# Dilated attention's values projected with tokens in the partitions, for several head pairs at once

## The chip, the cores and the metric

The kernel runs on one core of a Trainium2 chip. The metric is the device time of one execution in microseconds (us). Three runs of the kernel before gave 2261.0, 2262.21 and 2257.98; the median is 2261.0.

## The reference

Two decoder layers over 512 tokens of width 1024, in float32. Each layer is a half-step SwiGLU FFN, a token mixer and another half-step FFN, each between two RMSNorms and with shift, scale and gate computed from `c`. The first layer's mixer is latent attention; the second's is dilated attention, which the change is about:

```python
def dilated_attention(h, w_in, w_o, rel_bias):
    proj = (h @ w_in).reshape(B, S, N_GROUPS, 3, DIL_HEADS, DIL_HEAD_DIM)
    for g, (window, dilation) in enumerate(DIL_GROUPS):   # (128,1), (512,4), (2048,16)
        o, lse = strided_window_attention(
            proj[:, :, g, 0], proj[:, :, g, 1], proj[:, :, g, 2],
            dilation, window // dilation, rel_bias[:, g * DIL_HEADS:(g + 1) * DIL_HEADS])
    ...
    alpha = jax.nn.softmax(jnp.stack(lses, axis=0), axis=0)
    o = jnp.sum(alpha[..., None] * jnp.stack(outs, axis=0), axis=0)
    return o.reshape(B, S, DIL_WIDTH) @ w_o
```

There are three groups with 16 heads of 64 in each, every group with its own queries, keys and values. In group 0 a query sees the 128 tokens before it and itself, in group 1 every 4th token, in group 2 every 16th; a bias that depends on the distance is added to the scores. The three groups' results are joined by one softmax over all their scores.

## The kernel before, in words

The stages follow each other: FFN, latent attention, FFN, FFN, dilated attention (class `Dil`), FFN. All large products are made of three matmuls (`mm3`, L142): both operands are split into a part that TensorE's fp32r format holds and a rest, and high x high, high x low and low x high are added in PSUM. The lines L144, L145 and L146 are these three. A weight tile of 128x1024 is loaded by a DMA on SP's queue into one of 5 raw buffers, its high part is made by ACT (L129) and its rest by DVE in two halves (L131); `SLOTS` = 6 such pairs of tiles are in the ring.

The order of the instructions comes from a planner that estimates costs and puts each on its engine when it is ready, by its place in the program. Inside a `manual_schedule` block TensorE, ACT and DVE keep the order in which the program names them. SP's DMAs are always placed by the planner. The kernel has 44 SBUF tiles of 128x512 (`s`), four PSUM banks with the tag `mm` and four with `aux`. The normalized input `h` of a stage lies with the model dimension in the partitions and the 512 tokens along them, as 8 high and 8 low tiles. `x`, the residual stream, stays in SBUF the whole time (16 KB per partition).

The dilated stage goes by 8 pairs of heads. A pair has nine projections, one for each group and each of query, key and value (`tile`, L1032): 24 matmuls of 512 tokens, the weights being held in the array and `h` streaming, so that the result has the pair's 128 dimensions in the partitions. ACT copies it out of PSUM (L1061) and brings the tokens into the group's order; keys and values are written reversed (`back`), since the bias table is laid out for that. Products with the values need their tokens in the partitions. So every value tile is followed, one tile later, by four transposes of 128x128 on TensorE (L1071) and a copy by DVE (L1073).

One pair's attention stands beside the nine projections of the next pair (`slot`, L1279, and `beside`, L1300):

- slots 0 and 1: the scores (L1096) and, on DVE, bias and row minimum in one instruction (L1109). The minima of the three groups go out to DRAM and come back in another order (`tops_out`, L1135);
- tile 3: `tops` (L1142) joins them into one bound for all groups, which goes through DRAM again for groups 0 and 2;
- tiles 4 to 6: the exponentials and their sums on ACT (L1168), then the sums go through DRAM (`norm`, L1178);
- slots 7 and 8: transposes of group 0's weights (L1218) with their copies (L1230). Slot 0 of the next pair: those of group 1, and DVE's own 32x32 transposes for group 2 (L1232);
- slots 0 and 1 of the next pair: the products with the values (`weigh`, L1252), then the product with 1/sum (L1262), which comes by way of DRAM (`norm_out`, L1186).

`rest` (L1311) begins with the bias tables: a product (L971), a copy (L975), a DMA to DRAM (L976), and from there loads that put each head's table into a tile with shifted rows (L987). Pair 0's three value tiles follow, six other tiles having been made in the transition from the FFN before. `ahead` requests weights `LEAD` = 5 tiles in advance. At the end pair 7's scores come after the last tile, and the output projection (`part`, `tail`) runs beside its exponentials.

Of the kernel before, what the change touches and what calls it, by code (L numbers as in the profile page):

```python
# [14 lines left out]
P = 128  # L15
SEQ = 512
# [19 lines left out]
LEAD = 5  # L36
# [42 lines left out]
class Trunk:  # L79
    def __init__(self, ctx, tc, a):  # L80
# [11 lines left out]
        self.x = self.cp.tile([P, TT, D], F32, name="x")  # L92
# [14 lines left out]
        self.G = self.cp.tile([P, 2, 3, KT], F32, name="mG")  # L107

# [216 lines left out]
    def halves(self, i):  # L325
        return [self.x[:, i, d * SEQ : (d + 1) * SEQ] for d in range(2)]
# [10 lines left out]
    def start(self, sub):  # L337
# [16 lines left out]
        def stream(i):  # L354
            nc.sync.dma_start(self.x[:, i], self.a["x"][i])
# [137 lines left out]
    def tile_done(self, nxt, i):  # L493

        nc = self.nc
        r = self.scale_of(self.ss)
        for d in range(2):
            c = slice(d * SEQ, (d + 1) * SEQ)
            x = self.x[:, i, c]
# [22 lines left out]
class Ffn:  # L522
    heads = HEAD
    late = False
# [176 lines left out]
class Mla(Mixer):  # L701
    heads = 6
    late = True
# [245 lines left out]
class Dil(Mixer):  # L949
    heads = 6  # L950
    late = False
# [67 lines left out]
    ORDER = (0, 1, 3, 4, 6, 7, 2, 5, 8)  # L1019
# [12 lines left out]
    def tile(self, p, u, lo, hi):  # L1032
# [15 lines left out]
        if kind:  # L1048
            at = runs - at - part
        for q in range(1 if g < 2 else 4):  # L1050
            if g == 0:
                out, src = dst[:, at : at + part], b
            elif g == 1:
                out = dst.rearrange("p (r l) -> p r l", r=4)[:, :, at : at + part]
                src = self.order(b, 1)
            else:
                out = self.split(dst, 2)[:, q, :, at : at + part]
                src = self.order(b, 2)[:, q]
            if kind:
                src = self.back(src)  # L1060
            nc.scalar.activation(out, src, AF.Copy)  # L1061
# [15 lines left out]
    def scores(self, p, u, tag="mm"):  # L1077
# [26 lines left out]
        for e in range(2):  # L1104
            pair["y"][u, e] = y[e]
            at = 0
            for i, k0, n, b0 in blocks:
                c = slice(at, at + n)
                nc.vector.tensor_tensor_reduce(  # L1109
                    y[e][:, c],  # L1110
                    s[e][:, c],
                    pair["bias"][e][:, b0 : b0 + n],
# [110 lines left out]
    def turn_down(self, p, step, b):  # L1223
        t, nc = self.t, self.t.nc
        _, tag, pieces, _ = self.TURNS[step]
        out = self.pairs[p][step] = [t.t(tag) for e in range(2)]
# [7 lines left out]
    def weigh(self, p, step, first=0, last=3):  # L1234
# [5 lines left out]
        v = self.qkv[p, 3 * g + 2]  # L1240
        for nth, (kt, c0, n, at) in enumerate(products):
            for e in range(2):
# [6 lines left out]
                else:  # L1249
# [4 lines left out]
                    v[:, kt * P + 64 * e :][:, :64],  # L1254
# [5 lines left out]
        if step == last:  # L1260
            x = t.s()
            nc.vector.tensor_tensor(x, pair["acc"], pair["r"], ALU.mult)  # L1262
            self.of.append(x)

    def values(self, p, steps):
        for n in steps:
            self.weigh(p, n)

    def ahead(self, n):

        while self.coming and self.ahead_of < n:
            p, u = self.coming.pop(0)
            self.ahead_of += 1
            if p == "out":
                self.out_weights(u)
            else:
                self.wt[p, u] = self.t.weights(self.t.a["dil_in"][p, u])

    def slot(self, p, n):  # L1279

        if n == 0:
            if p:
                b = self.turn_up(p - 1, 2)
                self.values(p - 1, (0, 1))
            self.scores(p, 0)
            self.scores(p, 1)
            if p:
                self.turn_down(p - 1, 2, b)
                self.turn(p - 1, 3)
        elif n == 1:  # L1290
            if p:
                self.values(p - 1, (2, 3))
            self.scores(p, 2)
            self.scores(p, 3, "aux")
        elif n == 6:
            self.biases(p + 1)
        elif n > 6:
            self.turn(p, n - 7)

    def beside(self, p, n):  # L1300
        if n == 3:
            self.tops(self.pairs[p])
        elif n == 4:
            self.exps(p, (2,))
        elif n == 5:
            self.exps(p, (0, 1))
        elif n == 6:
# [3 lines left out]
    def rest(self):  # L1311
# [6 lines left out]
        tiles = [(0, u) for u in self.ORDER[6:]] + [(p, u) for p in range(1, 8) for u in self.ORDER]  # L1318
        self.coming = tiles + [("out", j) for j in range(PART)]
        self.ahead_of = 0  # L1320
        with t.tc.manual_schedule(engines={PE, ACT, DVE}):
            for at, (p, u) in enumerate(tiles):
                n = self.ORDER.index(u)
                if p:
                    self.slot(p - 1, n)
                if (p, n) == (7, 8):
                    self.scores(7, 0)
                self.ahead(at + LEAD)
                if p:
                    self.beside(p - 1, n)  # L1330
                self.tile(p, u, 0, SEQ)
                if p and n == 8:
                    self.norm_out(self.pairs[p - 1])
# [9 lines left out]
        self.scores(7, 2)  # L1343
        self.values(6, (2, 3))
        self.scores(7, 3)
# [3 lines left out]
        self.exps(7, range(4))  # L1349
        self.norm(self.pairs[7])  # L1350
        order = (2, 0, 1, 3)
        with t.tc.manual_schedule(engines={PE, DVE}):
# [9 lines left out]
            self.weigh(7, order[-1], order[0], order[-1])  # L1362
        self.put_o(self.of[-1])
# [29 lines left out]
def layout(i):  # L1393
# [52 lines left out]
    out["dil_in"] = tiles(w).reshape(8, 9, P, CH)  # L1446
    out["dil_o"] = c(g["dil_w_o"][0].reshape(KT, P, D))
# [31 lines left out]
```

## Time and profile before

| | |
|---|---|
| median of three runs | 2261.0 us |
| the profiled execution | 2258.17 us |
| its span, first to last instruction | 2256.1 us |
| granted TensorE clock, mean | 0.998 |
| TensorE busy in the span | 99% |
| DVE, ACT busy | 53%, 38% |
| transposes of value tiles (L1071) | 96, 14.6 us busy |
| DVE's copies behind them (L1073) | 24, 16.6 us busy |

A line of the view of groups names the source line, the engine, the operation, its output and inputs with the instruction's shape, and the count; then the busy time of the group, the mean time of one in ns, and the idle time of the engine before them with what ended it. `PE` is TensorE, `PEld` its weight load, which overlaps matmuls; matmuls are pipelined, so the distance from start to start says more than a duration. The chain of waits gives start, duration and the work that the end of the program hung on. A row of the stages has the window, its length, then busy time and count for PE, PEld, DVE, ACT and POOL, the granted clock, the share of the DMA engines and GB/s. `SPq` rows are DMAs as SP's queue issues them.

### The profile page before, as it was taken

The page shows a single profiled execution, that of the slowest core. Times are in us where ns is not written, and L with a number is a line of the kernel's source. Part 1 is how long each engine was busy: PE and PEld are TensorE (multiplying, and loading weights), DVE is VectorE, ACT ScalarE, POOL GpSimd, SP SyncE. Part 2 cuts the span into 40 slices and gives each one's busy share as a digit, 9 for nine tenths or more (in the row PEclk, how much of TensorE's full clock was granted, in tenths as well). Part 3 has the DMA queues.
Part 4 walks back from the last instruction along what each step waited for, and adds up shares of the span by engine and source line. Part 5 has one row for each costly group of instructions (what it writes and reads, how often), then busy time and mean ns, then how long its engine had stood idle before and what let it go on. Part 6 is the DMA issues. An engine that isn't in the chain of part 4 may idle for free.

```text
span 2256.1 us, 30214 instructions
## 1 busy us (share of the span) xinstructions
PE 2224.4 (99%) x11422; PEld 1853.9 (82%) x11422; DVE 1196.9 (53%) x2712; ACT 848.9 (38%) x1752; POOL 107.9 (5%) x143
## 2 busy tenths in 40 slices
PE   7999999999999999999999999999999999999998
PEld 5888888877898888898888888888888878888887
DVE  7666565677665356474554464343444467333344
ACT  4422234587633132353322252444444436322232
POOL 0000001210110000020000010000000002000000
PEclk9999999999999999999999999999999999999999
DMA  8575762311255365334553533333333322233231
GB/s 309 164 239 187 196 218 71 114 48 57 77 166 181 100 196 181 117 125 140 174 177 114 157 97 94 97 88 97 94 89 97 79 85 76 84 120 101 79 112 38
DMA packets 121224, 284.04 MB, mean 126 GB/s; under 512 B 44130, under 2 KB 48501, under 8 KB 121078
## 3 DMA queue, kind: packets, MB, share of 16 engines
q1 hardware_dynamic: 121078, 282.11, 41.0%
q8 instruction: 89, 1.46, 0.3%
q14 instruction: 57, 0.47, 0.1%
HBM read 279.67 MB, written 2.39 MB: 125 GB/s over the span
## 4 chain that ended last, share of the span: by engine, by line
PE 92%; issue 2%; ACT 2%; DVE 2%; DMA 1%; POOL 1%; SPq 0%; POOLq 0%; DVEq 0%; ACTq 0%
PE mm L144 28%; PE mm L145 28%; PE mm L146 28%; PE mm L863 1%; PE aux L1252 1%; PE mm L1096 1%; PE aux L1218 1%; PE aux L912 1%; POOL mv L319 1%; PE aux L891 1%; PE aux L513 1%; PE aux L1071 0%; ACT whi L129 0%; DVE x L500 0%; DMA d<-w 0%
## 5 line engine op out<-in xcount | busy, mean ns | idle before, releaser
L144 PE MATMUL mm<-s,whi 128*128 128x512 f32 (+1 forms) x2116 | 793.9, 376 | 2.7 <-ACT whi L129 2.4
L146 PE MATMUL mm<-s,wlo 128*128 128x512 f32 (+1 forms) x2116 | 790.0, 373 | 0.0
L145 PE MATMUL mm<-s,whi 128*128 128x512 f32 (+1 forms) x2116 | 790.0, 373 | 0.0
L131 DVE TENSOR_TENSOR wlo<-raw,whi 128x512 fp32r<-128x512 f32 (+1 forms) x712 | 466.6, 693 | 571.4 <-ACT whi L129 570.8
L129 ACT ACTIVATE whi<-raw 128x1024 fp32r<-128x1024 f32 (+1 forms) x356 | 369.1, 1052 | 789.4 <-PE mm L145 556.2
L144 PEld LDWEIGHTS mm<-s,whi 128*128 128x128 f32 x2116 | 398.4, 188 | 77.4 <-ACT whi L129 3.1
L146 PEld LDWEIGHTS mm<-s,wlo 128*128 128x128 f32 x2116 | 398.6, 188 | 70.8
L145 PEld LDWEIGHTS mm<-s,whi 128*128 128x128 f32 x2116 | 398.9, 189 | 68.7
L144 PE MATMUL mm<-whi,s 128*128 128x512 f32 x848 | 332.4, 392 | 2.8 <-DVE dm L1109 1.6
L145 PE MATMUL mm<-wlo,s 128*128 128x512 f32 x848 | 330.5, 390 | 0.0
L146 PE MATMUL mm<-whi,s 128*128 128x512 f32 x848 | 330.1, 389 | 0.0
L166 DVE CUSTOM_DVE_ANT_0 raw<-raw,cs 128x1024 f32<-128x1024 f32 x130 | 160.7, 1241 | 119.2 <-DMA raw<-w_mod 118.9
L144 PEld LDWEIGHTS mm<-whi,s 128*128 128x128 f32 x848 | 159.2, 188 | 37.0 <-issue 2.9
L146 PEld LDWEIGHTS mm<-whi,s 128*128 128x128 f32 x848 | 159.2, 188 | 33.3 <-issue 0.2
L145 PEld LDWEIGHTS mm<-wlo,s 128*128 128x128 f32 x848 | 159.2, 188 | 32.9 <-issue 0.5
L1061 ACT ACTIVATE s<-mm 128x512 f32<-128x512 f32 (+3 forms) x156 | 48.7, 370 | 261.4 <-PE mm L146 260.5
L460 DVE TENSOR_TENSOR s<-mm,s 128x512 f32<-128x512 f32 x112 | 76.7, 690 | 119.0 <-PE mm L146 118.8
L319 POOL TENSOR_TENSOR mv<-mv,mhalf 128x1 f32<-128x1 f32 x48 | 36.6, 763 | 1501.8 <-DVE mv L318 1499.3
L571 ACT ACTIVATE s<-gg 128x512 fp32r<-128x512 f32 (+1 forms) x97 | 57.4, 592 | 40.5 <-DVE gg L570 40.5
L570 DVE TENSOR_TENSOR gg<-silu,mm 128x512 f32<-128x512 f32 (+1 forms) x95 | 59.9, 630 | 10.3 <-ACT silu L568 10.3
L568 ACT ACTIVATE silu<-mm 128x512 f32<-128x512 f32 (+1 forms) x95 | 51.4, 541 | 15.8 <-PE mm L146 15.8
L145 PE MATMUL mm<-s 128*128 128x256 f32 (+1 forms) x176 | 52.9, 306 | 3.9 <-DVE s L308 2.3
(171 smaller groups left out, 1707.8 us busy)
## 6 DMA issues: line engine op xcount, KB each, us to landing
raw<-w_gu SPq DMA_DIRECT2D x168, 512.0 KB, 4.3
raw<-w_mod SPq DMA_DIRECT2D x130, 512.0 KB, 4.8
raw<-w_down SPq DMA_DIRECT2D x88, 512.0 KB, 4.3
raw<-dil_in SPq DMA_DIRECT2D x70, 512.0 KB, 3.7
s<-w_mod SPq DMA_DIRECT2D x28, 256.0 KB, 6.0
raw<-w_gu SPq DMA_DIRECT2D x16, 256.0 KB, 3.1
raw<-mla_o SPq DMA_DIRECT2D x8, 512.0 KB, 3.6
raw<-dil_o SPq DMA_DIRECT2D x8, 512.0 KB, 3.7
```

The source lines that it names most:

```text
L129: self.nc.scalar.activation(hi, raw, AF.Copy)
L131: self.nc.vector.tensor_tensor(lo[:, r], raw[:, r], f(hi[:, r]), ALU.subtract)
L144: mm(out, w[0], m[0], start=first, stop=False)
L145: mm(out, w[0], m[1], start=False, stop=False)
L146: mm(out, w[1], m[0], start=False, stop=last)
L166: nc.vector.tensor_tensor_reduce(raw, raw, self.cs, 1.0, 0.0, ALU.mult, ALU.add, accum_out=t[:, 0:1])
L319: nc.gpsimd.tensor_tensor(v[:, 1:2], v[:, 0:1], self.mhalf[:, 0:1], ALU.pow)
L460: nc.vector.tensor_tensor(y, b, y, ALU.add)
L568: nc.scalar.activation(s, banks[0], AF.Silu)
L570: nc.vector.tensor_tensor(v, s, banks[1], ALU.mult)
L571: nc.scalar.activation(ghi, v, AF.Copy)
L1061: nc.scalar.activation(out, src, AF.Copy)
```

## The change

Values of pairs 0 to 3 and of pairs 4 to 6 are projected together, with `h` held in the array as weights and the value weights streaming: for each group and each quarter of the tokens 24 matmuls over 512 or 384 columns. The result has its tokens in the partitions, and needs no transposes. For groups 1 and 2 the held operand is every 4th token of `h`; for group 2, four DMAs per quarter then bring the rows into the group's order. The twelve such tiles come behind the six query and key tiles that stand beside pair 0's and pair 4's attention. Pair 7's values are made as before, at the end.

The results need room: eight 128x512 pieces lie where `x` lies. `x` is now four tiles; in the transition to the dilated stage each is written to DRAM, and it is loaded back at the stage's end.

A pair's attention now stands beside six tiles. Values are no longer written reversed; DVE writes the scores reversed instead. All of `weigh` comes in slot 1, the transposes of groups 0 in slot 0 of the next pair.

```diff
-    ORDER = (0, 1, 3, 4, 6, 7, 2, 5, 8)
+    ORDER = (0, 1, 3, 4, 6, 7)
+    BLOCKS_V = {0: (0, 4), 4: (4, 7)}
+    LAST = (5, 2, 8)
...
+            if nxt.parks:
+                self.park(i)
+    def park(self, i):
+        to = self.parked[i] = self.dram.tile([P, D], F32, name=f"park{i}")
+        self.nc.sync.dma_start(to, self.x[i])
+    def unpark(self, i):
+        self.x[i] = self.wide()
+        self.nc.sync.dma_start(self.x[i], self.parked[i])
...
                 nc.vector.tensor_tensor_reduce(
-                    y[e][:, c],
-                    s[e][:, c],
-                    pair["bias"][e][:, b0 : b0 + n],
+                    self.back(o),
+                    a,
+                    b,
...
+    def keys_of(self, h, g, j):
+        return self.order(h, 1)[:, j] if g else h[:, j * P : (j + 1) * P]
+    def value_tile(self, p, g, j):
+        t, nc = self.t, self.t.nc
+        n = (self.BLOCKS_V[p][1] - p) * P
...
+        b = t.bank()[:, :n]
+        for k in range(KT):
+            w = [x[:, k % 2 * n :][:, :n] for x in self.wt[p, g, k // 2]]
+            h = [self.keys_of(x[k], g, j) for x in t.h]
+            t.mm3(b, h, w, k == 0, k == KT - 1)
+            if j == 3 and k % 2:
+                self.ahead(self.at + SLOTS + k // 2 + 1)
+        dst = self.made[g][j][:, :n]
+        out = t.s()[:, :n] if g == 2 else dst
+        nc.scalar.activation(out, b, AF.Copy)
+        if g == 2:
+            for a in range(4):
+                nc.sync.dma_start(
+                    dst[32 * a : 32 * a + 32], out.rearrange("(l a) v -> a l v", a=4)[a]
+                )
...
     def slot(self, p, n):
         if n == 0:
             if p:
-                b = self.turn_up(p - 1, 2)
-                self.values(p - 1, (0, 1))
+                up = [self.turn_up(p - 1, step) for step in range(2)]
+                for step in range(2):
+                    self.turn_down(p - 1, step, up[step])
             self.scores(p, 0)
             self.scores(p, 1)
             if p:
-                self.turn_down(p - 1, 2, b)
                 self.turn(p - 1, 3)
         elif n == 1:
+            if p == 7:
+                self.scores(p, 2)
+                self.scores(p, 3, "aux")
             if p:
-                self.values(p - 1, (2, 3))
-            self.scores(p, 2)
-            self.scores(p, 3, "aux")
-        elif n == 6:
+                for step in range(4):
+                    self.weigh(p - 1, step)
+            if p < 7:
+                self.scores(p, 2)
+                self.scores(p, 3, "aux")
+        elif n == 4:
             self.biases(p + 1)
-        elif n > 6:
-            self.turn(p, n - 7)
+        elif n == 5:
+            self.turn(p, 2)
     def beside(self, p, n):
-        if n == 3:
+        if n == 1 and p:
+            self.norm_out(self.pairs[p - 1])
+        elif n == 2 and p:
+            self.finish(p - 1)
+        elif n == 3:
             self.tops(self.pairs[p])
+            self.exps(p, (2,))
         elif n == 4:
-            self.exps(p, (2,))
-        elif n == 5:
             self.exps(p, (0, 1))
-        elif n == 6:
+    def behind(self, p, n):
+        if n == 5:
             self.exps(p, (3,))
             self.norm(self.pairs[p])
...
         with t.tc.manual_schedule(engines={PE, ACT, DVE}):
+            for p in range(7):
+                values = [(p, g, j) for g in range(3) for j in range(4) if p in self.BLOCKS_V]
+                for n, at in enumerate([(p + 1, u) for u in self.ORDER] + values):
+                    self.slot(p, n)
+                    self.ahead(self.at + min(SLOTS - 1 + max(n - 6, 0) % 4, SLOTS))
+                    self.beside(p, n)
+                    if n < 6:
+                        self.tile(*at, 0, SEQ)
+                    else:
+                        self.value_tile(*at)
+                    self.behind(p, n)
...
+            for n, u in enumerate(self.LAST):
+                self.slot(7, n)
+                self.ahead(self.at + SLOTS - 1)
+                self.beside(7, n)
+                self.tile(7, u, 0, SEQ)
...
         self.later()
-        b = self.turn_up(6, 2)
-        self.values(6, (0, 1))
-        self.turn_down(6, 2, b)
-        self.turn(6, 3)
-        self.scores(7, 1)
         for x in self.of[:PART]:
             self.put_o(x)
         t.new_y()
-        self.scores(7, 2)
-        self.values(6, (2, 3))
-        self.scores(7, 3)
         self.tops(self.pairs[7])
         for x in self.of[PART:]:
             self.put_o(x)
-        self.exps(7, range(4))
+        for i in range(TT):
+            t.unpark(i)
+        self.exps(7, (2, 0, 1, 3))
         self.norm(self.pairs[7])
```

More of the change, by code (lines that the diff above doesn't have):

```diff
@@ L702 @@
     heads = 6
+    parks = False
     late = True
@@ L950 @@
     heads = 6
+    parks = True
     late = False
@@ L1259, in weigh, with value @@
                 )
[L1260 to L1267, printed above, removed]
-    def ahead(self, n):
[L1271 to L1275, printed above, removed]
-            else:
-                self.wt[p, u] = self.t.weights(self.t.a["dil_in"][p, u])
+    def value(self, p, g, kt, e):
+        kt = kt if g else 3 - kt
+        if p == 7:
+            return self.qkv[p, 3 * g + 2][:, kt * P + 64 * e :][:, :64]
+        first = max(q for q in self.BLOCKS_V if q <= p)
+        return self.v[g][kt][:, (p - first) * P + 64 * e :][:, :64]
```

84 lines of the change are left out of this document (59 added, 25 removed).

## The prediction

> **What bounds the kernel now.** I read the page first, then busy times by stage, then the chain of waits, then single rows of the timeline.
>
> ```profile
> span 2256.1 us, 30214 instructions
> PE 2224.4 (99%) x11422; PEld 1853.9 (82%) x11422; DVE 1196.9 (53%) x2712; ACT 848.9 (38%) x1752; POOL 107.9 (5%) x143
> ```
>
> ```profile
> 1380.00:1820.00 440.00, 439.94 (x2478) 363.45 (x2478) 182.56 (x596) 179.24 (x541) 2.45 (x12) 1.00 0.35 92
> 1820.00:1830.00 10.00, 8.36 (x88) 6.95 (x85) 9.41 (x42) 1.43 (x3) 0.00 (x0) 1.00 0.25 78
> ...
> 1870.00:1880.00 10.00, 9.57 (x45) 7.56 (x44) 9.05 (x20) 8.21 (x21) 2.63 (x4) 1.00 0.39 107
> 1880.00:1890.00 10.00, 8.63 (x58) 7.40 (x59) 9.50 (x18) 9.80 (x23) 2.86 (x4) 1.00 0.30 103
> 1890.00:1900.00 10.00, 9.46 (x81) 9.23 (x80) 10.00 (x24) 8.18 (x19) 3.33 (x3) 1.00 0.48 145
> ```
>
> TensorE has work all the time; DVE and ACT are under half busy in the dilated stage (1380 to 1820: 182.56 and 179.24 of 440 us). So an instruction taken from TensorE there is worth its whole slot, one taken from DVE or ACT nothing, unless a wait changes. The only losses are at the end of the stage. One pair in the chain of waits:
>
> ```profile
> 1633.66 0.44 PE aux L1071 x4
> 1634.09 0.87 PE aux L1218 x8
> 1634.97 1.66 PE aux L1252 x16
> 1636.63 1.72 PE mm L1096 x16
> 1638.35 0.43 PE mm L144
> 1644.02 0.44 PE aux L1071 x4
> 1644.46 1.90 PE aux L1252 x32
> 1646.36 1.09 PE mm L1096 x16
> 1647.45 0.89 PE aux L1096 x16
> ...
> 1687.99 0.66 PE aux L1218 x6
> ...
> 1694.55 0.87 PE aux L1218 x8
> ```
>
> A pair takes 1694.55 - 1634.09 = 60.46 us. Every value tile ends in four transposes of 0.44 us, and they stand on the chain. The size of a slot comes from dense stretches:
>
> ```profile
> 1200.00:1300.00 100.00, 100.00 (x443) 82.77 (x442) 48.92 (x92) 26.29 (x33) 0.00 (x0) 1.00 0.50 138
> ```
>
> ```profile
> 1343.40 0.28 PE L145 MATMUL mm<-s 128*128 128x256 f32 x1
> 1343.52 0.28 PE L146 MATMUL mm<-s 128*128 128x256 f32 x1
> ```
>
> 443 matmuls with 512 columns in 100 us are 0.226 us each, and 256 columns take 0.12: 0.107 us per 256 columns and 0.013 per matmul. A matmul of 384 columns, not in the trace, should take 0.173.
>
> **The change, part by part.**
>
> Value projections. For 21 of 24 value tiles the four transposes go: 21 x 0.44 = -9.2 us. Their 21 copies out of PSUM leave DVE, which is worth nothing. The projection itself: pairs 0 to 3 had 4 x 3 x 24 = 288 matmuls of 512 columns and have 3 x 4 x 24 = 288 of 512, zero difference. Pairs 4 to 6 had 216 of 512 (48.8 us) and get 288 of 384 (49.8 us): +1.0 us.
>
> The new matmuls hold h as the weights, and for groups 1 and 2 a weight tile takes every 4th token of h: 2 x 2 x 96 = 384 weight loads with a step. What does the step cost? No load of the trace has one. Nearest rows:
>
> ```profile
> L144 PEld LDWEIGHTS mm<-whi,s 128*128 128x128 f32 x848 | 159.2, 188 | 37.0 <-issue 2.9 <-ACT s L695 1.6 <-DVE st L866 0.2
> L404 PEld LDWEIGHTS aux<-gb,s 1*128 1x128 f32 x4 | 1.2, 318 | 3.4 <-issue 3.4
> ```
>
> A packed load is shown at 188 ns, but loads overlap: with 256 columns a new one goes every 0.12 us. It may therefore grow to 0.226 before a 512-column matmul feels it and to 0.173 before a 384-column one. Lower bound: no cost, since packed loads are hidden already and a slower one cannot gain. Upper bound: the longest load of the trace, L404's 318 ns, 1.7 times 188; 1.7 x 0.12 = 0.203 costs 192 x 0.03 = 5.8 us in the second block alone. The nearest rows to a stepped access by TensorE stand in the chain above: L1252 x16 writes PSUM packed, 8 x 256 + 4 x 256 + 4 x 128 = 3584 columns (two passes per product) in 1.66 us; L1252 x32 writes every 4th or 16th place, 32 x 128 = 4096 columns in 1.90. Both are 0.46 ns per column: a step cost nothing there, so I take 0. The Trainium skill speaks against that: its page "PSUM — Partial Sum Buffer", Specifications (TRN2), says that a write pattern with gaps slows matmuls a lot; the two rows just given disagree (0.46 ns and 0.46). Its page "SBUF — State Buffer", Specifications (TRN2), says the same of reads from SBUF: below two hits in each 16-byte line a penalty is paid. No row here shows that for SBUF; by that rule the sum gets the first rival's price.
>
> The stage's beginning. Before, three value tiles of pair 0 (16 us) stand between the table matmuls and the first scores. They are gone: scores of pair 0 come first, and the loop issues the first weight subtractions behind them on DVE.
>
> ```profile
> 1377.10 2.10 PE L971 MATMUL aux<-s,u 33*16 33x384 f32 x6
> ```
>
> ```profile
> 1380.73 0.81 SPq L987 DMA_DIRECT2D s<-tv  x2
> ```
>
> ```profile
> L987 SPq DMA_DIRECT2D s<-tv x12: 318/414/422, 1380.7 to 1387.6; - x12
> ...
> DMA to landing us min/median/max: 1.6/1.7/3.1
> ```
>
> ```profile
> 1397.57 0.29 DVE L1109 CUSTOM_DVE_ANT_0 sq<-mm,s 128x128 f32<-128x128 f32 x1 [0.16 <-PE mm L1096]
> 1400.07 1.29 DVE L131 TENSOR_TENSOR wlo<-raw,whi 128x512 fp32r<-128x512 f32 x2
> ```
>
> TensorE would be through with tables and scores at 1377.10 + 2.10 + 1.72 = 1380.9. The first two bias loads (the ones that group 0 needs, 128 KB each, the largest) are issued from 1380.73 and take the longest of the landings, 3.1: 1383.8. The eight reductions take 1400.07 - 1397.57 = 2.5 us, the first half of the first subtraction 0.6 us (half of 1.29): 1386.9. The first projection can do two matmuls (0.45) before it needs that. So 1386.9 - 1380.9 - 0.45 = +5.5 us of a new wait. Behind it on DVE stand all weight subtractions, and TensorE waits for those; nothing covers it. At the shortest the weights' wait is hidden by an earlier load, and 3 us of bias latency stay; at the longest, third rival.
>
> The pair's order. Six tiles of 5.44 us are 32.6 us; with 60.46 - 9 x 5.44 - 3 x 0.44 = 10.2 us of attention a pair has 42.8 us for its round trips through DRAM, where it had 60.46. Scores end 14 us into the pair. Tops follow at tile 3 (about 28), the exponentials of group 1 need only them; those of group 0 need a further DRAM trip (some 6 us) and end near 38, before the next pair's first transposes at 42.8: 4.8 us of room (estimates from the rows above). The product with 1/z now waits on DVE at tile 2 for its own trip; behind it stand the subtraction for a weight tile four tiles later, which can wait, and the tops, for which the 28 already counts it. All transposes of group 0 and 2 then come first in the next pair, and DVE's four copies (2.1 us) stand ahead of the reductions that free the first bank: 14 transposes (1.53 us) go by meanwhile, so the bank is late by about 0.1 us per pair; one re-entry into the dense stream per pair is saved (0.43 against 0.226 in the chain). I set these two against each other: 0. Reversing the output of the reductions costs DVE at most some tenths there; DVE has room.
>
> Queues. SP gets four parks, four loads back and 32 small shuffles.
>
> ```profile
> raw<-dil_in SPq DMA_DIRECT2D x70, 512.0 KB, 3.7
> ```
>
> At about 3.7 us for 512 KB, and DMA busy 0.35 of the stage, they fit. A park waits for DVE's update of x, and loads of dil_in stand behind it on SP; five raw buffers are ahead of TensorE, so 0. Without that cover a park costs its 3.7 us. The values overwrite x only some 45 us later, and x is wanted back after the output projection: 0.
>
> The end.
>
> ```profile
> 1827.24 0.47 PE L144 MATMUL mm<-whi,s 128*128 128x512 f32 x1 [1.59 <-DVE dm L1109]
> 1863.78 0.50 PE L144 MATMUL mm<-whi,s 128*128 128x512 f32 x1 [1.19 <-ACT s L695]
> ```
>
> Pair 7's scores move ahead of two tiles, so its chain starts 11 us earlier: the second wait goes, -1.2 us. In the first one's place the first output part waits for ACT's copy of the last tile and the splitting of the first outputs, about as long: 0. The stage after it loses 0.43 + 1.37 + 0.54 = 2.3 us of busy time in 1870 to 1900; with the last pair's output on time that may halve: -1.0 (0 to -2.3).
>
> Sum: -9.2 + 1.0 + 5.5 - 1.2 - 1.0 = -4.9 us. The profiled execution took 2258.17 us (span 2256.1 and 2.1 around it); it would take 2253.3. The median of the runs, 2261.0, lies 2.8 above that execution, so I forecast 2261.0 - 4.9 = 2256.1.
>
> **The rivals.**
>
> First, ends slower: stepped weight loads take twice as long, 0.24 us start to start instead of 0.12. Then 192 loads cost 0.24 - 0.226 = 0.014 in the first block, 2.7 us, and 192 cost 0.067 in the second, 12.9 us: -4.9 + 15.6 = +10.7, 2271.7. It decides from 0.173 us per load on. For it: packed loads have little room in the second block; against it: the PSUM rows. The factor of two is my estimate; the rule behind it is the one cited above from the Trainium skill's page on SBUF. Chance 0.18.
>
> Second: the room of 4.8 us per pair isn't there, because SP stands at a raw load while the trip of the tops is due.
>
> ```profile
> 1656.99 5.76 SPq L121 DMA_DIRECT2D raw<-dil_in  x2
> ```
>
> Such a stand of 5.8 us leaves TensorE 1 us short, with a second delayed trip more; for the six pairs 8 us: 2264.1. Against it: this stand ended when the tops were ready. Chance 0.14.
>
> Third: the opening wait is longer, because a reduction waits for the whole bias tile, whose last load lands at 1387.6 + 1.7 = 1389.3 instead of 1383.8: +5.5, 2261.6, no change. A wait of over 5 us could also cost clock. In 1820 to 1830 a gap of 1.59 us left it at 1.00. The Trainium skill, page "TensorE: Matmul & The Clock Gate", Part 1, says that an idle window of some 3.4 us halves it for another; that would be an estimated 1.7 us more, and no row here shows it. Chance 0.10.
>
> Fourth: the opening wait does not come (the tables are computed among the earlier tiles, since their inputs were there): 2250.6. Chance 0.08.
>
> **How the numbers follow.** Forecast 0.50. Its own range is 2252 (wait of 3 us, 2.3 regained at the end, rest unchanged) to 2261; somewhat over two thirds of it lie below 2256.5. With 0.2%, 4.5 us, as what a measurement can tell from no change: faster 0.34 + 0.08 = 0.42; same 0.15 and half of the second and third rival, 0.27; slower 0.31. The range goes from 2250 to 2272: it takes in all five cases, and leaves out a weight load slower than twice, and a sum of rivals.
>
> **What would show it.** L1071 with 12 transposes instead of 96. TensorE idle near 1381 to 1387, ended by DVE's wlo or dm. L144's matmuls with 384 columns 0.173 us apart, whether h is read packed or every 4th token: a larger distance with the step proves the first rival. Pairs without values 42.8 us apart: longer means the second. If TensorE's count falls as worked out and the time does not, the lost time must stand as idle before a line of the pair.

## The result and the profile after

The changed kernel takes 2277.86 us (median of 4 runs, 2275.93 to 2278.56) against 2261.61 for the kernel before: the ratio is 1.0074, 95% interval 1.0056 to 1.0091. It is slower by 16 us, where 2256.1 was forecast. Two executions lie far above all others (3707.8 us of the kernel before, 4511.74 us of e10_parks_twice below) and are left out throughout. The page of the profiled execution:

```profile
span 2276.0 us, 30275 instructions
...
PE 2236.2 (98%) x11410; PEld 1879.6 (83%) x11410; DVE 1184.7 (52%) x2697; ACT 849.8 (37%) x1737; POOL 105.0 (5%) x143
...
L148 PEld LDWEIGHTS mm<-whi,s 128*128 128x128 f32 x1040 | 212.4, 204 | 37.2 <-ACT s L711 1.8
```

TensorE was to lose work and is busy 11.8 us longer (2224.4 before); and a weight load with `h` or another activation as the held operand has gone from 188 to 204 ns in the mean. The lines of the new code are shifted: `mm3` is L148 to L150, weight splits L133 and L135 (also the name of the reductions), scores L1118, transposes of probabilities L1244 with copies L1256, products L1277. The value transposes are gone as planned, 12 instead of 96 (the view of groups):

```profile
L1093 PE MATMUL aux<-ident,s 128*128 128x128 f32 x12 | 2.0, 290 | 0.7 <-ACT s L1083 0.7
```

The stages, in the columns of the prediction's table (PE, PEld, DVE, ACT, POOL, clock, DMA share, GB/s):

```profile
1380.00:1400.00 20.00, 15.58 (x89) 11.57 (x87) 13.64 (x61) 1.65 (x2) 0.41 (x2) 0.83 0.49 152
...
1440.00:1460.00 20.00, 20.00 (x87) 18.83 (x86) 5.18 (x8) 6.52 (x8) 0.00 (x0) 1.00 0.32 105
1480.00:1500.00 20.00, 17.95 (x93) 16.81 (x93) 10.58 (x30) 5.92 (x7) 0.00 (x0) 1.00 0.46 145
1660.00:1680.00 20.00, 20.00 (x110) 19.09 (x109) 4.01 (x9) 8.57 (x30) 0.00 (x0) 1.00 0.48 91
1680.00:1700.00 20.00, 20.00 (x90) 20.00 (x90) 4.01 (x8) 4.40 (x7) 0.00 (x0) 1.00 0.30 99
...
1720.00:1740.00 20.00, 17.95 (x90) 15.50 (x91) 11.00 (x30) 5.62 (x7) 0.41 (x2) 0.91 0.40 125
1840.00:1850.00 10.00, 8.15 (x31) 5.74 (x30) 6.29 (x10) 9.47 (x34) 0.00 (x0) 0.83 0.78 255
```

Two kinds of loss are seen. From 1680 to 1700 PE is never idle, but in 20 us it does only 90 matmuls of 384 columns: 0.222 us each in the mean (the first 2 us are still packed), not 0.173, and PEld is full. And there are four places with idle time, three of them with a lower clock (0.83, 0.91, 0.83): the opening, the ends of the two value blocks, the end of the stage.

**The stepped loads.** Single matmuls of pairs 4 to 6, in the timeline; first where `h` is read packed (group 0), then every 4th token:

```profile
1669.76 0.33 PE L150 MATMUL mm<-whi,s 128*128 128x384 f32 x1
...
1670.63 0.33 PE L149 MATMUL mm<-wlo,s 128*128 128x384 f32 x1
```

```profile
1699.63 0.39 PE L149 MATMUL mm<-wlo,s 128*128 128x384 f32 x1
...
1700.80 0.39 PE L148 MATMUL mm<-whi,s 128*128 128x384 f32 x1
```

Five starts apart: 0.87 / 5 = 0.174 us packed, 1.17 / 5 = 0.234 stepped. With 512 columns it is 0.227 and 0.235. So with the step a matmul can start only every 0.233 to 0.235 us, whether it has 384 columns or 512. What sets that distance is the load, and PEld is busy all the time there (20.00 of 20 us).

**The opening**, in the chain of waits:

```profile
1378.65 2.04 PE aux L989 x6
1380.68 0.85 PE mm L1118 x8
1381.53 3.11 DMA s<-tv
1384.78 0.25 DVE sq L1135
...
1387.36 0.61 DVE wlo L135
1388.02 0.80 PE mm L150
1388.81 0.43 PE mm L148
1389.24 0.43 PE mm L149
```

The wait is the one forecast: tables, 3.11 us of bias load, reductions, then the first subtraction. Behind it matmuls go every 0.43 us instead of 0.227, until 1391.4.

**The ends of the value blocks**, which the prediction doesn't mention (chain, first block):

```profile
1492.21 1.07 ACT whi L133
...
1493.30 1.29 DVE wlo L135 x2
1494.60 1.20 DVE silu L1256 x2
1495.80 0.93 DVE gg L1256 x2
...
1496.93 0.34 DVE sq L1135
...
1497.42 0.47 PE mm L148
```

The next tile's first matmul needs a bank; the scores hold it till the reductions have read it; ahead of those stand on DVE the weight split that `ahead` issues behind the last matmuls of the block, and four copies of turned probabilities. From the start of the last score to the start of that matmul pass 2.43 us, 2.05 of them idle. The second block ends alike, and there the next matmuls go at 0.43 us until 1736:

```profile
1732.16 0.47 PE mm L148
...
1733.16 0.43 PE mm L148
...
1735.72 0.43 PE mm L148
```

Between pairs without values the same place takes 0.52 us.

**The pairs** without values are as long as forecast, 42.85 us from transposes to transposes:

```profile
1536.89 1.53 PE aux L1244 x14
...
1579.74 1.53 PE aux L1244 x14
...
1622.57 1.53 PE aux L1244 x14
```

**The end:**

```profile
1839.53 1.94 ACT u L1194 x10
...
1841.99 1.06 ACT whi L133
1843.05 0.59 ACT s L1083 x4
...
1844.67 0.53 ACT s L711
1845.25 0.57 PE mm L148
1845.82 0.43 PE mm L149
```

The last tile's matmuls are through near 1842. On ACT the planner has put a weight copy (L133), itself behind eight exponentials of pair 7, ahead of that tile's copy (L1083), and two more exponentials ahead of the first outputs' split (L711). The gaps are 0.97 and 1.48 us from start to start, then the clock is half.

### The profile page after: what moved, and what is told of

It reads as the page before. It is cut to its first block, busy times and chain, and to the rows that moved or that the text cites. A ratio compares the mean times of both kernels' runs of the same rounds, so it can differ in the third digit from the quotient of the medians.

```text
span 2276.0 us, 30275 instructions
## 1 busy us (share of the span) xinstructions
PE 2236.2 (98%) x11410; PEld 1879.6 (83%) x11410; DVE 1184.7 (52%) x2697; ACT 849.8 (37%) x1737; POOL 105.0 (5%) x143
## 4 chain that ended last, share of the span: by engine, by line
PE 91%; DVE 3%; ACT 2%; issue 2%; POOL 1%; DMA 1%; POOLq 0%; DVEq 0%; SPq 0%; ACTq 0%
PE mm L148 28%; PE mm L149 28%; PE mm L150 28%; PE mm L880 1%; PE aux L1277 1%; PE mm L1118 1%; PE aux L929 1%; PE aux L1244 1%; POOL mv L323 1%; PE aux L908 1%; DVE wlo L135 1%; PE aux L528 1%; ACT whi L133 0%; DVE x L504 0%; PE aux L1118 0%
## 5 line engine op out<-in xcount | busy, mean ns | idle before, releaser
L135 DVE TENSOR_TENSOR wlo<-raw,whi 128x512 fp32r<-128x512 f32 (+2 forms) x718 | 467.6, 689 | 591.6 <-ACT whi L133 589.6
L148 PE MATMUL mm<-s,whi 128*128 128x512 f32 (+1 forms) x1948 | 730.4, 376 | 9.8 <-DVE dm L1135 7.3
L150 PE MATMUL mm<-s,wlo 128*128 128x512 f32 (+1 forms) x1948 | 726.2, 373 | 1.3 <-DVE wlo L135 1.3
L149 PE MATMUL mm<-s,whi 128*128 128x512 f32 (+1 forms) x1948 | 726.3, 373 | 0.0
L133 ACT ACTIVATE whi<-raw 128x1024 fp32r<-128x1024 f32 (+2 forms) x359 | 369.4, 1044 | 810.1 <-PE mm L149 548.1
L148 PEld LDWEIGHTS mm<-s,whi 128*128 128x128 f32 x1948 | 368.1, 189 | 78.8 <-issue 9.8
L150 PEld LDWEIGHTS mm<-s,wlo 128*128 128x128 f32 x1948 | 368.2, 189 | 66.3 <-DVE wlo L135 2.0
L149 PEld LDWEIGHTS mm<-s,whi 128*128 128x128 f32 x1948 | 368.7, 189 | 62.7
L148 PE MATMUL mm<-whi,s 128*128 128x512 f32 (+1 forms) x1040 | 406.9, 391 | 1.2 <-ACT s L711 1.2
L149 PE MATMUL mm<-wlo,s 128*128 128x512 f32 (+1 forms) x1040 | 405.1, 390 | 0.0
L150 PE MATMUL mm<-whi,s 128*128 128x512 f32 (+1 forms) x1040 | 404.7, 389 | 0.0
L148 PEld LDWEIGHTS mm<-whi,s 128*128 128x128 f32 x1040 | 212.4, 204 | 37.2 <-ACT s L711 1.8
L150 PEld LDWEIGHTS mm<-whi,s 128*128 128x128 f32 x1040 | 212.5, 204 | 35.1 <-DVE s L712 1.0
L149 PEld LDWEIGHTS mm<-wlo,s 128*128 128x128 f32 x1040 | 212.5, 204 | 34.2 <-issue 0.7
L1083 ACT ACTIVATE s<-mm 128x128 f32<-128x128 f32 (+3 forms) x114 | 34.4, 358 | 182.4 <-PE mm L150 178.5
L586 DVE TENSOR_TENSOR gg<-silu,mm 128x512 f32<-128x512 f32 (+1 forms) x95 | 59.9, 630 | 10.5 <-ACT silu L584 10.5
```

The lines of the kernel that those rows point to most:

```text
L133: self.nc.scalar.activation(hi, raw, AF.Copy)
L135: self.nc.vector.tensor_tensor(lo[:, r], raw[:, r], f(hi[:, r]), ALU.subtract)
L148: mm(out, w[0], m[0], start=first, stop=False)
L149: mm(out, w[0], m[1], start=False, stop=False)
L150: mm(out, w[1], m[0], start=False, stop=last)
L586: nc.vector.tensor_tensor(v, s, banks[1], ALU.mult)
```

## The experiments

To see the terms apart from the scatter of the stages around, the stage is measured in the trace of each run (one execution) from the first transposes of `h` in the transition into it to the first in the transition out of it. Before this takes 545.58 us, after 562.37: +16.8. What precedes it differs by up to 2.9 us among the changed kernels, which agree there; what follows takes 373.4 us before and 375.0 in every changed kernel. (Of the 19.9 us between the two spans, 1.5 lie ahead of the stage and are scatter; the medians differ by 16.3.)

| run | median us | ratio to before, 95% interval | stage us | stage against after |
|---|---|---|---|---|
| after | 2277.86 | 1.0074, 1.0056 to 1.0091 | 562.37 | |
| e1_packed | 2267.45 | 1.0035, 1.0020 to 1.0049 | 551.73 | -10.6 |
| e2_early_tables | 2273.03 | 1.0056, 1.0041 to 1.0071 | 556.25 | -6.1 |
| e3_late_weight | 2274.29 | 1.0064, 1.0049 to 1.0079 | 558.50 | -3.9 |
| e4_step2 | 2271.09 | 1.0048, 1.0033 to 1.0063 | 554.45 | -7.9 |
| e5_tail | 2275.28 | 1.0073, 1.0058 to 1.0088 | 560.87 | -1.5 |
| e6_natural | 2266.41 | 1.0033, 1.0021 to 1.0044 | 549.75 | -12.6 |
| e8_scores_first | 2273.94 | 1.0064, 1.0047 to 1.0080 | 558.59 | -3.8 |
| e7_all | 2249.87 | 0.9964, 0.9951 to 0.9977 | 536.07 | -26.3 |
| e9_best | 2247.39 | 0.9945, 0.9932 to 0.9958 | 533.58 | -28.8 |
| e10_parks_twice | 2248.46 | 0.9949, 0.9933 to 0.9965 | 532.69 | -29.7 |
| e11_transposes_back | 2257.90 | 0.9992, 0.9983 to 1.0002 | 543.10 | -19.3 |

The next table cuts the stage at the same matmuls in every trace and gives the difference to the changed kernel (after) in us. "Behind" a block is from its last matmul to the 31st matmul of the key and query tiles that follow; the end begins with the last matmul of the last projection.

| run | up to the first value block | the two value blocks | behind the first | behind the second | other pairs | end |
|---|---|---|---|---|---|---|
| e1_packed | +0.1 | -13.1 | 0.0 | +0.3 | 0.0 | +2.0 |
| e2_early_tables | -6.1 | 0.0 | +1.6 | -1.6 | 0.0 | 0.0 |
| e3_late_weight | +0.1 | 0.0 | -1.4 | -3.0 | +0.1 | +0.4 |
| e4_step2 | -0.2 | -11.8 | +1.6 | +0.4 | 0.0 | +2.0 |
| e5_tail | +0.4 | 0.0 | +1.6 | -1.6 | +0.1 | -2.0 |
| e6_natural | +0.1 | -13.1 | 0.0 | +0.4 | 0.0 | -0.1 |
| e8_scores_first | +0.3 | 0.0 | -2.1 | -3.7 | -0.8 | +2.5 |
| e7_all | -5.3 | -13.1 | -1.4 | -2.3 | -0.1 | -4.1 |
| e9_best | -6.4 | -13.1 | -2.1 | -3.8 | -0.9 | -2.7 |

Each repair acts in its own part. What moves besides is the end and the half clock: in e2 and e5 the latter went from behind the second block to behind the first (+1.6 and -1.6).

The theory: the change's gain is there, and is outweighed by stepped weight loads and by waits at the seams of the new order. Rivals: that only the clock or the transfers matter, or that the loads are slow for their size and not for their step.

**e1_packed: the held operand without a step**

```diff
-        return self.order(h, 1)[:, j] if g else h[:, j * P : (j + 1) * P]
+        return h[:, j * P : (j + 1) * P]
```

> The changed kernel with one line of it altered: for groups 1 and 2 the held operand is 128 neighbouring tokens of h instead of every 4th one. Which tokens land in which value tile is thereby changed, the amount of work is not. Theory (the step in the weight load costs): in the trace of the changed kernel the stepped matmuls start 0.233 us apart with 384 columns, where packed ones start 0.173 apart, and 0.233 against 0.227 with 512. So 192 x 0.060 + 192 x 0.006 = 12.7 us fewer, near 2265, and 0.173 and 0.227 in all three groups. Rival (the distance comes from late weights or from 384 columns as such): no change, near 2278.

(The values then belong to other tokens, so the result is another; the work is the same. That holds for e4_step2 too.)

Measured: 10.4 us less in the median, 10.6 in the stage, and all matmuls 0.227 and 0.173 us apart. So the step is the cause, not the size of the load. The two blocks themselves are 13.1 us shorter; 2.3 of that is given back, since the waits behind grow: 2.43 to 2.91 us at the second block's end, 1.48 to 3.13 at the stage's end.

**e4_step2: every 2nd token**

```diff
-        return self.order(h, 1)[:, j] if g else h[:, j * P : (j + 1) * P]
+        if not g:
+            return h[:, j * P : (j + 1) * P]
+        return h[:, j // 2 * HT :][:, :HT].rearrange("p (l r) -> p r l", r=2)[:, j % 2]
```

> As e1, but the held operand of groups 1 and 2 is every 2nd token of h (8 bytes apart) instead of every 4th (16 bytes apart); again other tokens in the tiles, the same amount of work. Theory by the Trainium skill's page on SBUF (full speed from two hits in each 16-byte line on): as packed, 0.173 us apart with 384 columns, 12 us fewer, near 2265. First rival (any step costs the same): 0.233 apart, near 2278. Second rival (cost grows with the step): 0.20 or so, near 2272.

```profile
1691.80 0.34 PE L150 MATMUL mm<-whi,s 128*128 128x384 f32 x1
...
1692.50 0.34 PE L148 MATMUL mm<-whi,s 128*128 128x384 f32 x1
```

In the timeline of this run, four starts apart, 0.70 / 4 = 0.175 us with 384 columns: as packed. With 512 columns some 0.233 stay, against 0.227; why, no run shows. The Trainium skill, page "SBUF — State Buffer", Specifications (TRN2), wants two hits in each 16-byte line for full bandwidth: floats 8 bytes apart give that, floats 16 bytes apart don't. The 384-column rows agree (0.175 and 0.234); the 512-column ones show a smaller cost that this rule doesn't give. The stage gains 7.9 us, less than expected, though the two blocks gain 11.8: the rest is given back behind them, by half clock after the first block too and by a longer end.

**e2_early_tables: tables and first biases among the tiles of the transition**

```diff
+        if lo and u == 1:
+            self.bias = {}
+            self.tables()
+            self.biases(0)
         self.tile(0, self.ORDER[u], lo, hi)
...
-        self.bias = {}
-        self.tables()
-        self.biases(0)
...
+            self.ahead(SLOTS - 1)
```

> The changed kernel with the bias tables and pair 0's biases asked for in the middle of the six tiles that are made in the transition, and the first five weight tiles split ahead of the first scores instead of behind them. Theory (the opening wait is the biases' trip through DRAM with the weight subtraction queued behind it on DVE, and the half clock after it): the gap of 3.5 and 1.9 us goes, and the eight matmuls that start 0.43 us apart start 0.227 apart: 5.4 + 1.6 = 7.0 us fewer, near 2271. Rival (the biases are late for another reason, their own slots or SP): under 2 us.

```profile
1380.00:1400.00 20.00, 20.00 (x129) 16.76 (x128) 9.25 (x54) 4.77 (x13) 0.41 (x2) 1.00 0.28 81
```

In this window of its stages PE isn't idle any more and the clock is 1.00. 4.8 us in the median, 6.1 in the stage: (3.54 - 0.43) + (1.88 - 0.43) = 4.6 us of idle time, and about eight matmuls that took 0.2 us too long. (The opening itself is 6.8 us shorter; the transition, where the table products now stand, is 0.6 longer.) The earlier tables and the earlier weight splits are one edit here; what each gives alone wasn't run.

**e3_late_weight and e8_scores_first: two ways to shorten DVE's queue at the block ends**

```diff
-            if j == 3 and k % 2:
+            if j == 3 and k % 2 and (g, k) != (2, KT - 1):
```

> The changed kernel, without the request of the next weight tile behind the very last products of a block of values; the next slot asks for it instead. Theory (that tile's high part waits for TensorE's last matmul of the block, its rest stands on DVE ahead of the four copies and of the reductions that free the first bank): the two gaps of 2.43 us at the ends of the blocks shrink to the 0.52 us of the other pairs, and the half clock behind the second goes: 2 x 1.9 + 1.6 = 5.4 us fewer, near 2272. Rival (the four copies alone make the bank late): the gaps stay, no change.

```diff
-                for step in range(2):
-                    self.turn_down(p - 1, step, up[step])
             self.scores(p, 0)
             self.scores(p, 1)
             if p:
+                for step in range(2):
+                    self.turn_down(p - 1, step, up[step])
                 self.turn(p - 1, 3)
```

> The changed kernel with one order changed on VectorE: at the start of a pair the eight reductions of the first scores come ahead of the four copies of turned probabilities (L1256) instead of behind them. Theory (the first matmul behind the scores waits for its bank, which is late because the copies stand ahead of the reductions: 0.52 us from start to start where the kernel before has 0.25, and 2.4 us where a value block has just ended): 0.25 us in each of five pairs and up to 0.9 us at each of two block ends, and the half clock behind the second: 2277.9 - 1.2 - 1.8 - 1.5 = 2273.4 us. Rival (at the block ends it is the weight split's subtraction on VectorE that is late, not the copies; and the products then wait for the copies): 2276.5 us or more, the block-end gaps still over 2 us.

e3 gives 3.6 us in the median, 3.9 in the stage, less than expected: the gap goes from 2.43 to 1.02 us, not to 0.52. e8 gives 3.9 and 3.8, and no start-to-start distance over 0.43 us is left, neither at the block ends nor between pairs. By the table of parts that is 6.6 us at these seams, the half clock behind the second block included, of which 2.5 are lost again at the stage's end, where its second gap is 2.72 us instead of 1.48 and more matmuls go at half clock. Its chain at the first block's end:

```profile
1492.33 1.53 PE aux L1244 x14
1493.85 1.72 PE mm L1118 x16
1495.57 0.43 PE mm L148
```

So neither instruction alone is the cause: 1.29 us of split and 2.13 us of copies stand in one queue ahead of the reductions, and TensorE's own 14 transposes and 16 scores cover part of it. To take the split away ends most of the wait, to move the copies behind the reductions all of it.

**e5_tail: another order at the end**

```diff
+                if n == 2:
+                    for x in self.of[:PART]:
+                        self.put_o(x)
                 self.tile(7, u, 0, SEQ)
...
+                if n == 0:
+                    self.later()
```

(The second piece is behind the first `part`; ScalarE's exponentials of pair 7 are written behind the last tile's copy.)

> The changed kernel with another end of the attention stage: the high and low parts of the first three outputs (L711, L712) are made in front of the last value tile instead of behind it, its four turning transposes (L1093) come behind the first output product, and ScalarE's order at the end is written out, so that the exponentials of pair 7 no longer stand ahead of the last tile's copy. Theory (an end that was not foreseen: the last tile's copy and put_o behind eight exponentials and a weight copy): the two gaps of 0.97 and 1.48 us behind the last tile and the eleven matmuls at half clock behind them, some 2 us, go; 2277.9 - 4.4 = 2273.5 us, and TensorE's matmuls stand 0.227 us apart through 1842 to 1850. Rival (the same time is given back at the stage's last wait, since pair 7's exponentials and sums now end later and its last product waits for them; or the gap is simply a clock matter): 2277 to 2279 us, with a new gap before L1277 near 1863 or 1880.

Mostly a miss: 2.6 us in the median, 1.5 in the stage. The gaps at 1842 go, and two others come, 0.80 and 0.93 us; the second in the chain:

```profile
1851.86 2.50 DVE s L712 x4
1854.36 0.61 DVE s L466
...
1855.01 0.50 PE mm L148
```

The copy that frees the bank of an output product (L466) now stands on DVE behind four splits. The rival was right in that time is given back, though at another place than it said.

**e6_natural: packed loads, the same result**

```diff
-        return self.order(h, 1)[:, j] if g else h[:, j * P : (j + 1) * P]
+        return h[:, j * P : (j + 1) * P]
...
+        if g == 1:
+            for r in range(4):
+                nc.sync.dma_start(
+                    self.made[g][r][32 * j : 32 * j + 32, :n],
+                    out.rearrange("(l r) v -> r l v", r=4)[r],
+                )
...
+            nc.sync.dma_start(self.mixed[j * P : (j + 1) * P], out)
...
+            rows = self.mixed.rearrange("(l a j) v -> j a l v", a=4, j=4)
+            for i in range(4):
+                for a in range(4):
+                    nc.sync.dma_start(self.made[g][i][32 * a : 32 * a + 32, :n], rows[i, a])
```

> The changed kernel, computing the same thing, with every value weight load packed: the four value tiles of groups 1 and 2 take 128 neighbouring tokens each, and are put into their places of every fourth or sixteenth token behind TensorE, group 1 by 16 SBUF to SBUF transfers of 32 rows, group 2 by 4 writes to DRAM and 16 reads. The groups go in the order 2, 1, 0, so that the transfers lie under the tiles of the next group. Theory (the every-fourth-token weight load is the largest mis-sized term, 192 loads of 512 columns by 0.008 and 192 of 384 columns by 0.060 us): as packing alone did with other tokens, 10.4 us less than the changed kernel: 2267.5 us, 0.227 and 0.173 us from start to start in all twelve tiles. Rival (the transfers cost what the packing gains: products wait for rows that land late, or SP's queue holds up the weights): 2274 us or more, with idle time of TensorE at the products (L1277) of pairs 1 and 5 or before a value tile.

11.5 us less in the median, 12.6 in the stage, at 0.173 us with 384 columns; no product waits for a row. The two blocks are 13.1 us shorter, and the count gives the same: 192 x 0.0085 + 192 x 0.060 = 13.1.

**e7_all: four repairs together**

> The changed kernel, computing the same thing, with four repairs at once: packed value weight loads as in the run beside it, tables and first biases ahead of the stage, no weight split behind the last matmuls of a value block, the other end of the stage. Theory (the four costs found are all that separates the change from its sum; the rest of the prediction's steps stand): 2277.9 - 10.4 - 4.8 - 3.6 - 4.4 = 2254.7 us by addition of the single runs, and by the prediction's own sum against the kernel before 2259.7 - 9.2 + 1.0 - 1.2 - 1.0 = 2249.3 us, so 2249 to 2256, faster than the kernel before by 4 to 10 us. Rival (the repairs overlap or a further cost of the parks, of the transfers or of the late reductions stays): 2259 us or more, no gain on the kernel before.

2249.87 us, below the addition (2254.7) and near the prediction's own sum without the wait at the opening (2249.3). The stage is 26.3 us shorter; e2, e3, e5 and e6 alone add up to 24.1. The 2.2 more stand at the end, which is 4.1 us shorter, where e5 alone had 2.0: the two waits that e5 had brought in don't appear here.

```profile
1680.00:1700.00 20.00, 20.00 (x118) 20.00 (x117) 4.55 (x8) 6.13 (x9) 0.41 (x2) 1.00 0.32 100
1700.00:1720.00 20.00, 18.67 (x150) 16.14 (x151) 9.53 (x28) 5.60 (x7) 0.00 (x0) 1.00 0.46 159
```

Packed, 118 matmuls go where 90 went, 0.17 us each. What is left stands in the second row: 1.70 us at the second block's end, with the copies still ahead of the reductions.

**e9_best: e8's order added.** It is faster than both kernels.

> The changed kernel, computing the same thing, with five repairs: the four of the run e7_all (2249.9 us) and the reductions of a pair's first scores ahead of the copies of its turned probabilities on VectorE. Theory (what is left of idle time in that run's values stage, 0.52 us behind the scores of five pairs and 1.06 and 1.70 us at the two block ends, is due to those copies, and falls to 0.25 us each): 2249.9 - 5 x 0.27 - 0.81 - 1.45 = 2246.3 us. Rival (with the weight split already gone the block-end wait has another cause, or the products then wait for the copies): 2249 to 2251 us.

2247.39 us (2245.50 to 2249.32), 0.55% below the kernel before; the stage 2.5 us shorter than in e7_all, of 3.6 expected. The seams give 2.9 and the way up to the first block 1.0, but the end is 1.5 longer: one of e5's waits is back, 0.96 us of idle time with L466 behind four splits on DVE.

```profile
1821.69 2.50 DVE s L712 x4
1824.19 0.61 DVE s L466
...
1824.85 0.50 PE mm L148
```

The page and the second block's end:

```profile
span 2245.6 us, 30319 instructions
...
PE 2214.0 (99%) x11410; PEld 1854.6 (83%) x11410; DVE 1183.5 (53%) x2697; ACT 849.7 (38%) x1737; POOL 107.7 (5%) x143
```

```profile
1700.00:1720.00 20.00, 20.00 (x165) 16.97 (x163) 13.05 (x61) 5.11 (x6) 0.00 (x0) 1.00 0.37 123
```

**e10_parks_twice and e11_transposes_back: two of the prediction's terms by themselves**

```diff
-        self.nc.sync.dma_start(to, self.x[i])
+        for _ in range(2):
+            self.nc.sync.dma_start(to, self.x[i])
...
-        self.nc.sync.dma_start(self.x[i], self.parked[i])
+        for _ in range(2):
+            self.nc.sync.dma_start(self.x[i], self.parked[i])
```

> The run e9_best with each of the four tiles of x written to DRAM twice and read back twice: eight transfers of 512 KB more on SP's queue. Theory (the prediction's zero for parks and unparks: they lie under other work at both ends): no change from e9_best, within 0.2%. Rival (a transfer of 512 KB takes SP's queue and the channels some 4 us, and at the stage's start the value weights, at its end the last products stand behind it): 3 to 16 us more.

```diff
+        if kind == 0 and p:
+            def again():
+                x = t.bank("aux")
+                for j in range(4):
+                    r = slice(j * P, (j + 1) * P)
+                    nc.tensor.transpose(x[:, r], dst[:, r], t.ident)
+                nc.vector.tensor_copy(t.s(), x)
+            self.later = again
```

> The run e9_best with the 21 groups of four transposes put back that the change had removed: behind the copies of 21 query tiles four transposes of the copied tile into a bank, and a VectorE copy of it that nothing reads. Theory (the prediction's first term, 0.44 us for each group and its copy beside other work): 9.2 us more than e9_best, 2255.5 if that gives 2246.3. Rival (a group costs more than its four starts, since TensorE changes over between the kinds of matmul, 0.1 to 0.2 us each time, or waits for a bank): 11 to 14 us more; or less than 6, if the transposes ran beside waits.

Against e9_best the doubled parks give +1.1 us in the median, 0.05%, and -0.9 in the stage: nothing. The transposes give +9.5 us in the stage, 0.453 for each group, and 10.5 in the median.

## Why the prediction was wrong

By its steps, each in the stage's time:

- **Transposes, -9.2:** right, 9.5 (e11).
- **288 matmuls of 384 columns, +1.0:** right where `h` is packed, 0.174 against 0.173.
- **Step of the weight loads, taken as 0 (bounds 0 to 5.8): the step that failed.** It costs 13.1 us in the two value blocks (e1 and e6; 12.6 in e6's whole stage), outside the bounds. The value was taken from the products that write PSUM with a step at 0.46 ns per column. That is the nearest row in form, but another path: an output, where the held operand is an input from SBUF. And the upper bound came from a load of one partition, L404, with no step. The first rival had it right: 0.24 us from start to start assumed, 0.234 measured; 15.6 us forecast, 13.1 measured. The rule behind it, from the Trainium skill's page "SBUF — State Buffer", Specifications (TRN2), is about the memory that the held operand is read from; the rival was given 0.18.
- **Opening, +5.5:** right in mechanism and nearly in size, 6.1 (e2). 4.6 of it is idle time; the other 1.6 or so is the half clock that the third rival had as an estimate of 1.7. The longer wait of that rival, for the whole bias tile, did not come: the first reduction started at 1384.78.
- **Pair order, 0:** the period was right (42.85), the seams were not. The sum let the transposes cover the copies, and did not list what else stands on DVE behind a value block, the weight split. The block ends cost 5.8 us, 1.6 of it half clock, and the other pairs 0.8 in all, 0.17 each where 0.1 was set off against a gain: 6.6 us (e8). No rival had the block ends.
- **Parks, queues, 0:** right (e10). The second rival, a pair without room, did not come.
- **End:** the second wait is gone, as forecast. The wait "about as long" in place of the first is longer: 0.97 and 1.48 us and half clock against 1.86 us once. Against the end of e7_all, which has no such wait, it costs 4.1 us, half clock included; the one wait of before, 1.86 us where 0.23 is the rule, cost 1.6.
- **Next stage, -1.0:** +1.6, within its first 15 us, in e9_best as in the rest; so it doesn't come from the last output being late; and reading `x` back twice (e10) leaves it the same. No run took it apart: its cause stays open.

The range ended at 2272 us, just above the first rival's 2271.7, and left out a sum of rivals by intent. What came was that rival's step, and beside it the seams and the end, which were set at 0 and which no rival priced.

The terms -9.2, +1.0 and -1.2 make 536.2 us of the 545.58, and e7_all, with the step and most waits repaired, takes 536.07. That they meet so closely is partly luck: in e7_all some waits are left at the seams, and e9_best takes 533.58, 2.6 us less than these terms give; where that comes from, no run shows. The gain was there at least in the size forecast. The changed kernel stands 28.8 us above e9_best in this stage: 13.1 for the step, 6.4 up to the first block, 6.7 at the seams and 2.7 at the end.

## What to carry to other kernels

A stepped operand is priced by a row of the same path (held, streamed or written), and where none exists, by the rule that speaks of that path; here it also had a cure, to read packed and let DMAs reorder the result behind other work. At every seam of a new order, write down each instruction that stands on the helping engine ahead of the one that frees the bank, also those that come from prefetching. And to put repairs together before the change is given up: each alone was still slower than before, all together faster.

## What was not expected of the hardware

A weight load of 128 columns of floats 16 bytes apart takes about 0.233 us, against 0.12 or less packed (256-column matmuls start that far apart); 8 bytes apart costs nothing that 384-column matmuls feel.

The clock halved after idle times that are shorter than thought: behind the 2.43 us at 1732 (2.05 of them idle) matmuls were 0.43 us apart for some 3.4 us, behind the same 2.43 us at 1497 not. In e2_early_tables and e5_tail it was the other way round, half clock behind the first block and none behind the second. At the stage's end gaps of 0.97 and 1.48 us, with four transposes between them, were followed by it too. The Trainium skill, page "TensorE: Matmul & The Clock Gate", Part 1, has a free-running window of 3.4 us, so that the phase decides. The varying phase agrees; that a window must be idle as a whole doesn't, with gaps of 2.43 us. A wait of 2.4 us was thus worth up to 1.6 us more than it shows.
